# Differential attention: second softmax scaled by ScalarE and added by GpSimd, reciprocals by GpSimd, the output's transpose a stage later; band attention: one reciprocal per job

## The chip, the cores and the metric

The kernel runs on one core of a Trainium2 chip. The metric is device time in microseconds of one launch, as the median of several runs. A profile is one further execution, recorded instruction by instruction. The engines are TensorE (PE, with its weight loads PEld), VectorE (DVE), ScalarE (ACT), GpSimd (POOL) and SyncE (SP), which issues nearly all transfers. Each engine works through its own queue in order; semaphores tie the queues together.

## The reference

One encoder layer on x of shape (1, 1024, 1024) in float32. A half-step feed-forward comes first, then a mixer with two attention branches and gates, then a second half-step feed-forward and a norm. The change touches only the two attention branches. What they compute, cut to what matters:

```python
# band branch: 8 heads of 64, chunks of 64, own chunk and 8 to the left
sc = einsum(q, k) * d**-0.5 + bias          # band of 576 keys per chunk
p  = softmax(sc);  o = p @ v

# differential branch: 4 heads, two score maps each, 8 blocks of 128 queries
sc   = einsum('bqhrd,bkhrd->bhrqk', q, k) * d**-0.5 + t5_bias, chunk-causal
p    = softmax(sc)
attn = p[:, :, 0] - lam * p[:, :, 1]
o    = attn @ v                              # 128 value columns
o    = rms_norm(o, subln_g) * (1 - lambda_init)
```

## The kernel before

The feed-forwards and projections are matrix products in a Strassen-like form (seven products for eight), in a high and a low part of float32r each; they fill the time before 1077 us and after 1357 us. The attention lies between them, in one PSUM pool: two score tiles (`sc`, two banks each), two transpose tiles (`pt`), two result tiles (`pv`).

Attention work is cut into jobs. A band job is one head and two query blocks; 32 of them run first. A differential job is one head and one query block `i`, whose score width is `(i + 1) * 128`, from 128 to 1024 columns; 32 of them follow, 4 heads of 8 blocks. A job is a generator, and `run` (L811) steps the jobs as a pipeline: at each step a new job does its scores and softmax, the job of two steps before does its transposes, the one of three steps before its value product, and the one of four steps before its output transpose. The step only sets the order of the program text. The framework plans each engine's queue from that order, from what is ready in its own timing model, and from free buffers: a tile tag with `bufs=n` has n buffers, and an instruction that needs a new one cannot go into the queue before an old one is free.

A differential job before the change, line by line. L779/L780 are the two score products (high query times high and low keys). L787 adds the bias on VectorE and takes the row minimum, L789 is ScalarE's exp with the row sum `rs`. L922 and L924 are the reciprocals r1 and r2 on VectorE, L925 turns r2 into minus lambda times rs0/rs1, and L927 adds the second exp tile, scaled by r2, to the first. Two stages later L795 transposes the tile block by block, L97 (ScalarE) and L102 (VectorE) split it into high and low part (`whi`, `wlo`), and L943/L944 multiply with the values. L946 and L948 (ScalarE) take the two halves out of PSUM, scaled by r1; L949 (GpSimd) adds them to o1; L952 (VectorE) sums the squares; L139 (GpSimd) takes the power -1/2 and L955 (GpSimd) makes a diagonal `dg` of it. One stage later L958 multiplies o1 with dg on TensorE, which transposes and scales at once, and L99/L104 split the result into `y`.

A filler runs in between: every second job also does one 512-column piece of the band branch's output projection (`pb`, L128 to L130, times a gate tile `gl` in L892, stored by L893). The next head's queries, keys and values (`load_qkv`, L757) are loaded into the "big" buffers when the old ones come free.

The band job has the same softmax, then per query block a reciprocal on VectorE (L847) and a product with it on GpSimd (L848).

## Time and profile before

| | |
|---|---|
| median of 3 runs | 2159.53 us (2156.72 to 2159.69) |
| profiled execution | 2157.48 us, span of its instructions 2155.1 us |
| TensorE, VectorE, ScalarE, GpSimd busy | 96%, 68%, 45%, 9% of the span |
| band attention | about 1077 to 1187 us |
| differential attention | about 1187 to 1357 us |

Busy time is the time in which at least one instruction of the engine was under way. Matmuls overlap in the pipeline, so a busy TensorE isn't one at full pace. A wait names the instruction that waited and the one that released it.

### The profile page before, as it was taken

The numbers are of one execution on the slowest core, as the hardware profiler recorded it, in microseconds if no ns is written. First come the engines' busy times: TensorE is split into PE (matmuls) and PEld (weight loads), VectorE is DVE, ScalarE is ACT, GpSimd is POOL, SyncE is SP. The second block draws the span as 40 slices with busy tenths as digits, with TensorE's granted clock in tenths as the row PEclk, the third lists the DMA queues.
The fourth block names the chain that finished last, engine by engine and source line by source line (L and its number), as shares of the span: only waits on it lengthen the run. The fifth ranks groups of instructions, "written<-read, shape, count | busy, mean of one in ns | idle before, by whom it ended". The sixth has DMA issues, their size and how long they took to land.

```text
span 2155.1 us, 29016 instructions
## 1 busy us (share of the span) xinstructions
PE 2074.9 (96%) x10025; PEld 1730.3 (80%) x10025; DVE 1460.8 (68%) x2678; ACT 975.0 (45%) x1911; POOL 193.3 (9%) x290
## 2 busy tenths in 40 slices
PE   6999999999999999999999988898999999999997
PEld 5788888888888788899788877776788888888886
DVE  7666566577577756566488877777766656658566
ACT  5433333334446544444498665135433333334444
POOL 2120000000001000000066233201000000000001
PEclk9999999999999999999999999999999999999999
DMA  6653333294345544553682365614643333366344
GB/s 193 174 169 111 96 95 118 93 336 133 118 130 158 169 143 164 195 196 137 224 279 103 134 210 184 230 59 157 181 156 92 114 94 96 114 244 220 98 118 156
DMA packets 277572, 333.55 MB, mean 155 GB/s; under 512 B 15421, under 2 KB 168013, under 8 KB 277425
## 3 DMA queue, kind: packets, MB, share of 16 engines
q1 hardware_dynamic: 276096, 327.94, 46.8%
q0 software_dynamic: 1184, 3.24, 0.6%
q8 instruction: 79, 1.29, 0.3%
q14 instruction: 69, 0.56, 0.1%
q10 hardware_dynamic: 144, 0.52, 0.1%
HBM read 226.45 MB, written 105.19 MB: 154 GB/s over the span
## 4 chain that ended last, share of the span: by engine, by line
PE 80%; DVE 7%; DMA 5%; ACT 4%; issue 3%; SPq 1%; POOL 0%; ACTq 0%; DVEq 0%; POOLq 0%
PE prod L128 19%; PE prod L129 19%; PE prod L130 18%; PE po L129 6%; PE po L130 6%; PE po L128 6%; DVE wlo L102 2%; ACT whi L97 1%; ACT pm L789 1%; PE tr L205 1%; PE pb L128 1%; PE pb L130 1%; PE pb L129 1%; PE pt L795 1%; PE sc L779 1%
## 5 line engine op out<-in xcount | busy, mean ns | idle before, releaser
L129 PE MATMUL po<-wlo,whi 128*128 128x512 f32 x728 | 285.2, 392 | 5.5 <-DVE wlo L102 5.4
L130 PE MATMUL po<-whi,wlo 128*128 128x512 f32 x728 | 283.9, 390 | 0.0
L97 ACT CAST whi<-raw 128x512 fp32r<-128x512 f32 x200 | 124.4, 622 | 311.5 <-PE prod L129 244.4
L97 ACT CAST whi<-T 128x512 fp32r<-128x512 f32 x196 | 121.9, 622 | 249.7 <-PE prod L129 228.5
L97 ACT CAST whi<-B 128x512 fp32r<-128x512 f32 x178 | 110.8, 623 | 266.1 <-PE po L129 258.2
L113 DVE TENSOR_TENSOR c<-prod,c 128x512 f32<-128x512 f32 x190 | 131.1, 690 | 133.3 <-PE prod L130 122.3
L102 DVE TENSOR_TENSOR wlo<-raw,whi 128x512 fp32r<-128x512 f32 x200 | 138.6, 693 | 106.2 <-ACT whi L97 64.8
L102 DVE TENSOR_TENSOR wlo<-B,whi 128x512 fp32r<-128x512 f32 x178 | 122.4, 688 | 127.3 <-ACT whi L97 127.3
L128 PE MATMUL po<-whi 128*128 128x512 f32 x728 | 198.8, 391 | 0.4 <-DVE xc L507 0.3
L102 DVE TENSOR_TENSOR wlo<-T,whi 128x512 fp32r<-128x512 f32 x196 | 134.6, 687 | 92.5 <-ACT whi L97 91.6
L139 POOL TENSOR_TENSOR r<-v,neg_half 128x1 f32<-128x1 f32 x64 | 50.3, 790 | 1324.2 <-DVE v L180 1225.9
L129 PEld LDWEIGHTS po<-wlo,whi 128*128 128x128 f32 x728 | 136.9, 188 | 38.0 <-DVE wlo L102 9.8
L128 PEld LDWEIGHTS po<-whi 128*128 128x128 f32 x728 | 136.7, 189 | 29.9 <-ACT whi L97 1.4
L130 PEld LDWEIGHTS po<-whi,wlo 128*128 128x128 f32 x728 | 136.9, 188 | 28.2
L102 DVE TENSOR_TENSOR wlo<-N,whi 128x512 fp32r<-128x512 f32 x64 | 44.1, 689 | 113.2 <-PE prod L129 62.9
L102 DVE TENSOR_TENSOR wlo<-ha,whi 128x512 fp32r<-128x512 f32 x154 | 105.4, 684 | 9.0 <-ACT whi L97 9.0
L272 ACT COPY c<-prod 128x512 f32<-128x512 f32 x186 | 103.1, 586 | 11.2 <-DMA hA<-c 4.3
L97 ACT CAST whi<-ha 128x512 fp32r<-128x512 f32 x154 | 94.8, 615 | 16.9 <-PE prod L129 11.4
L789 ACT ACTIVATE pm<-pm,mn 128x640 f32<-128x640 f32 (+7 forms) x128 | 94.0, 736 | 11.9 <-DVE ri L924 6.3
L128 PE MATMUL prod<-A11h,whi 128*128 128x512 f32 x240 | 95.7, 399 | 2.6 <-ACT A11h L97 2.6
L128 PE MATMUL prod<-S1h,whi 128*128 128x512 f32 x240 | 94.1, 392 | 3.1 <-ACT S1h L97 2.1
L787 DVE CUSTOM_DVE_ANT_0 pm<-sc,nb 128x640 f32<-128x640 f32 (+7 forms) x128 | 87.9, 698 | 12.5 <-PE sc L780 5.9
(246 smaller groups left out, 5369.4 us busy)
## 6 DMA issues: line engine op xcount, KB each, us to landing
raw<-in_ffn_w_in_dram SPq DMA_DIRECT2D x98, 512.0 KB, 4.4
raw<-in_w_mix_in_dram SPq DMA_DIRECT2D x47, 512.0 KB, 4.5
ha<-hS SPq DMA_DIRECT2D x88, 256.0 KB, 2.7
hA<-c SPq DMA_DIRECT2D x66, 256.0 KB, 4.3
ha<-hA SPq DMA_DIRECT2D x66, 256.0 KB, 2.7
B<-in_ffn_w_out_dram SPq DMA_DIRECT2D x12, 1024.0 KB, 10.3
hS<-hs SPq DMA_DIRECT2D x44, 256.0 KB, 3.0
hS<-c SPq DMA_DIRECT2D x44, 256.0 KB, 4.5
```

The costliest lines, as they stand in the source:

```text
L97: nc.scalar.copy(out=hi, in_=src)
L102: (nc.gpsimd if on_pool else nc.vector).tensor_tensor(out=lo, in0=src, in1=h, op=ALU.subtract)
L113: nc.vector.tensor_tensor(out=out_, in0=a, in1=b, op=op)
L128: nc.tensor.matmul(ps, a[0], b[0], start=first, stop=False, skip_group_check=shared)
L129: nc.tensor.matmul(ps, a[0], b[1], start=False, stop=False, skip_group_check=shared)
L130: nc.tensor.matmul(ps, a[1], b[0], start=False, stop=last, skip_group_check=shared)
L139: nc.gpsimd.tensor_tensor(out=r, in0=v, in1=neg_half, op=ALU.pow)
L205: nc.tensor.transpose(tr[:, k, :], rows[:, k * P:(k + 1) * P], ident)
L272: nc.scalar.copy(out=self.held[name], in_=p)
L779: nc.tensor.matmul(sc[:, m, :wc], qs[:, h, c], ks[:, h, kc], start=True, stop=False)
L787: nc.vector.tensor_tensor_reduce(out=d3, in0=sc, in1=nb.rearrange("p (n w) -> p n w", n=n), scale=1.0, scalar=3e38, op0=ALU.add, op1=ALU.m ...
L789: nc.scalar.activation(out=dst, in_=dst, func=AF.Exp, bias=mn, scale=-1.0, accum_out=rs)
```

## The change

In the differential branch the two row sums share one tile, and one GpSimd instruction raises both to the power -1 (instead of two VectorE reciprocals). ScalarE scales the second exp tile by r2 in place and GpSimd adds it to the first (instead of one fused VectorE instruction). The reciprocals get a tag of their own with 6 buffers. The output's transpose (L958) moves one stage later, by a second `yield`, and `run` keeps five jobs alive instead of four. In the band branch the two row sums share a tile and are inverted by one VectorE reciprocal behind the second softmax; both GpSimd products follow it.

```diff
+    neg_one = const.tile([P, 2], F32, name="neg_one")
+    nc.vector.memset(neg_one, -1.0)
...
-            for step, job in enumerate(list(jobs) + [None] * 4):
+            for step, job in enumerate(list(jobs) + [None] * 5):
                 for g in [job] + live[::-1] if job else live[::-1]:
                     next(g, None)
-                live = (live + [job] if job else live)[-4:]
+                live = (live + [job] if job else live)[-5:]
...
+                rs = small.tile([P, 2], F32, tag="rs", bufs=4, name="rs")
                 for s, i in enumerate((i0, i1)):
                     w = (i - first[s] + 1) * P
                     sc, n = scores(qkv, h, i, first[s] * P, w)
                     pm = raw_tile([P, D], "pm")[:, :w]
-                    rs = small.tile([P, 1], F32, tag="rs", name="rs")
-                    softmax(sc, n, nb[:, h, WA - w:WA], pm, rs)
-                    ri = small.tile([P, 1], F32, tag="ri", name="ri")
-                    nc.vector.reciprocal(out=ri, in_=rs)
-                    nc.gpsimd.tensor_tensor(out=pm, in0=pm, in1=ri.to_broadcast([P, w]), op=ALU.mult)
+                    softmax(sc, n, nb[:, h, WA - w:WA], pm, rs[:, s:s + 1])
                     pms.append(pm)
+                ri = small.tile([P, 2], F32, tag="ri", name="ri")
+                nc.vector.reciprocal(out=ri, in_=rs)
+                for s, pm in enumerate(pms):
+                    nc.gpsimd.tensor_tensor(out=pm, in0=pm, in1=ri[:, s:s + 1].to_broadcast(list(pm.shape)), op=ALU.mult)
...
-                pr, rs = [], []
+                pr = []
+                rs = small.tile([P, 2], F32, tag="rs", name="rs")
                 for r in range(2):
                     sc, n = scores(qkv, r, i, 0, w)
                     pm = raw_tile([P, WB], "pm")[:, :w]
-                    s_ = small.tile([P, 1], F32, tag="rs", name="rs")
-                    softmax(sc, n, nb[:, WB - w:], pm, s_)
+                    softmax(sc, n, nb[:, WB - w:], pm, rs[:, r:r + 1])
                     pr.append(pm)
-                    rs.append(s_)
-                r1, r2 = (small.tile([P, 1], F32, tag="ri", name="ri") for _ in range(2))
-                nc.vector.reciprocal(out=r1, in_=rs[0])
-
-                nc.vector.reciprocal(out=r2, in_=rs[1])
-                nc.vector.scalar_tensor_tensor(out=r2, in0=r2, scalar=neg_lam, in1=rs[0],
+                ri = small.tile([P, 2], F32, tag="rj", bufs=6, name="ri")
+                nc.gpsimd.tensor_tensor(out=ri, in0=rs, in1=neg_one, op=ALU.pow)
+                r1, r2 = ri[:, 0:1], small.tile([P, 1], F32, tag="r2", name="r2")
+
+                nc.vector.scalar_tensor_tensor(out=r2, in0=ri[:, 1:2], scalar=neg_lam, in1=rs[:, 0:1],
                                                op0=ALU.mult, op1=ALU.mult)
-                nc.vector.scalar_tensor_tensor(out=pr[0], in0=pr[1], scalar=r2, in1=pr[0],
-                                               op0=ALU.mult, op1=ALU.add)
+                nc.scalar.activation(out=pr[1], in_=pr[1], func=AF.Copy, scale=r2)
+                nc.gpsimd.tensor_tensor(out=pr[0], in0=pr[0], in1=pr[1], op=ALU.add)
...
                 dg = small.tile([P, P], F32, tag="dg", bufs=2, name="dg")
                 nc.gpsimd.tensor_tensor(out=dg, in0=ident, in1=rsqrt(v).to_broadcast([P, P]), op=ALU.mult)
+                yield
                 yield
                 tr = ps.tile([P, 4, P], F32, tag="pt", bufs=2, name="try")
```

## Rows read from the trace of the kernel before

**Rows 1.** The page's busy time by engine: microseconds, share of the span, instructions.

```profile
PE 2074.9 (96%) x10025; PEld 1730.3 (80%) x10025; DVE 1460.8 (68%) x2678; ACT 975.0 (45%) x1911; POOL 193.3 (9%) x290
```

**Rows 2.** Busy time by stretch: the band part and the differential part. Columns: stretch, its length, then busy time (and instructions) of TensorE, its weight loads, VectorE, ScalarE and GpSimd, the granted TensorE clock (1.00 is 2.4 GHz), the DMA share and GB/s.

```profile
1077.00:1187.00 110.00, 102.33 (x734) 91.33 (x735) 96.92 (x311) 98.21 (x255) 74.21 (x93) 1.00 0.56 189
...
1187.00:1357.00 170.00, 147.02 (x872) 126.85 (x871) 133.51 (x410) 101.79 (x274) 55.64 (x100) 0.97 0.55 185
```

**Rows 3.** Waits of TensorE in the differential part: who waited for whom, microseconds in total, times, longest.

```profile
PE try L958 <- POOL dg L955: 4.6, 4, 2.4
PE pv L943 <- ACT o L948: 3.2, 6, 0.9
PE sc L779 <- DVE mn L787: 2.8, 5, 1.2
PE sc L779 <- DMA ks<-k: 2.2, 1, 2.2
PE pb L128 <- DVE gl L892: 2.2, 2, 1.6
PE try L958 <- DVE wlo L102: 2.1, 2, 1.8
PE try L958 <- DVE ri L925: 2.0, 2, 1.1
```

**Rows 4.** Waits of VectorE and ScalarE around the reciprocals, in the differential part.

```profile
ACT pm L789 <- DVE ri L924: 6.3, 9, 1.8
...
DVE ri L924 <- ACT o L948: 4.8, 5, 1.4
```

**Rows 5.** The end of the differential part in order of time, engine by engine: start, duration, engine, line, operation, tiles, shapes; in brackets the idle time before it and its releaser.

```profile
1330.89 0.19 ACT L789 ACTIVATION_READ_ACCUMULATOR pm<-pm,mn 128x1 f32 x1
...
1335.51 0.15 DVE L924 RECIPROCAL ri<-rs 128x1 f32<-128x1 f32 x1
1338.01 0.69 DVE L892 TENSOR_TENSOR gl<-pb,gl 128x512 f32<-128x512 f32 x1 [2.35 <-DMA gl<-g]
...
1339.55 1.27 DVE L927 SCALAR_TENSOR_TENSOR pm<-pm,ri 128x1024 f32<-128x1024 f32 x1
...
1353.90 0.49 PE L958 MATMUL try<-dg,o 128*128 128x128 f32 x2 [2.42 <-POOL dg L955]
```

**Rows 6.** VectorE's groups in the differential part, by shape: busy microseconds and mean ns of one, then idle time before them. L927 has eight widths of 4 jobs each (one of the narrowest lies before the stretch); the widest and the narrowest are shown.

```profile
L925 DVE SCALAR_TENSOR_TENSOR ri<-ri,neg_lam,rs 128x1 f32<-128x1 f32 x30 | 6.8, 227 | 0.2
...
L927 DVE SCALAR_TENSOR_TENSOR pm<-pm,ri 128x1024 f32<-128x1024 f32 x4 | 5.1, 1275 | 0.0
...
L922 DVE RECIPROCAL ri<-rs 128x1 f32<-128x1 f32 x30 | 4.7, 157 | 0.3
L924 DVE RECIPROCAL ri<-rs 128x1 f32<-128x1 f32 x30 | 4.6, 155 | 4.9 <-ACT o L948 4.8
...
L927 DVE SCALAR_TENSOR_TENSOR pm<-pm,ri 128x128 f32<-128x128 f32 x3 | 1.2, 394 | 0.0
```

**Rows 7.** ScalarE: the exp at its widest and narrowest in the differential part (busy, mean ns, idle before), and the one scaled copy from SBUF to SBUF in the program (a group over the whole span: shortest, median and longest ns, first and last start).

```profile
L789 ACT ACTIVATE pm<-pm,mn 128x1024 f32<-128x1024 f32 x8 | 9.2, 1147 | 1.1 <-DVE ri L924 0.9 <-DVE mn L787 0.2
...
L789 ACT ACTIVATE pm<-pm,mn 128x128 f32<-128x128 f32 x6 | 2.4, 404 | 1.6 <-DVE mn L787 1.6
...
L197 ACT ACTIVATE xc<-xc,r x12: 705/712/730, 682.1 to 2148.4; 128x512 f32<-128x512 f32 x12
```

**Rows 8.** GpSimd over the whole span: instructions with two tiles as input, by shape (busy, mean ns, idle before), and the power on one column (shortest, median and longest ns, first and last start).

```profile
L949 POOL TENSOR_TENSOR o<-o,o 128x128 f32<-128x128 f32 x32 | 14.7, 460 | 60.6 <-ACT o L948 60.6
L102 POOL TENSOR_TENSOR y<-ysum,y 128x256 fp32r<-128x256 f32 x16 | 11.8, 737 | 23.6 <-ACT y L97 23.6
...
L1000 POOL TENSOR_TENSOR mS<-mA,tA 128x512 f32<-128x512 f32 x4 | 5.5, 1386 | 22.5 <-DVE tA L113 22.5
...
L139 POOL TENSOR_TENSOR r<-v,neg_half x64: 544/560/2061, 7.4 to 2147.3; 128x1 f32<-128x1 f32 x64
```

**Rows 9.** The band part: the reciprocal (shortest, median and longest ns, first and last start) and TensorE's largest wait there.

```profile
L847 DVE RECIPROCAL ri<-rs x64: 144/158/166, 1078.7 to 1175.2; 128x1 f32<-128x1 f32 x64
...
PE pt L795 <- DVE wlo L102: 4.8, 15, 0.5
```

**Rows 10.** Two places of the differential part in order of time where GpSimd and VectorE meet: columns as in rows 5.

```profile
1291.81 0.45 POOL L949 TENSOR_TENSOR o<-o,o 128x128 f32<-128x128 f32 x1 [1.36 <-ACT o L948]
...
1291.96 0.32 DVE L925 SCALAR_TENSOR_TENSOR ri<-ri,neg_lam,rs 128x1 f32<-128x1 f32 x1
...
1332.86 1.15 DVE L927 SCALAR_TENSOR_TENSOR pm<-pm,ri 128x896 f32<-128x896 f32 x1
...
1333.02 1.40 POOL L139 TENSOR_TENSOR r<-v,neg_half 128x1 f32<-128x1 f32 x1 [0.41 <-DVE v L952]
```

**Rows 11.** Loads of a head's keys in the differential part: count, KB each, median microseconds from issue to landing.

```profile
ks<-k SPq DMA_DIRECT2D x3, 1024.0 KB, 8.9
kl<-kx SPq DMA_DIRECT2D x3, 1024.0 KB, 11.6
```

## The prediction

> **What bounds the kernel now.** I read the page's busy shares first: TensorE (PE) works 96% of the span and VectorE (DVE) 68% [rows 1]. As a mean over the whole program this says that TensorE is the limit, and that VectorE relief is worth little. The change touches only the attention part, so I next read the busy time by stretch [rows 2]. The band part (1077 to 1187 us) has TensorE at 102.3 of 110.0 us, ScalarE at 98.2 and VectorE at 96.9: three engines near their limit, 7.7 us of TensorE idle. The differential part (1187 to 1357 us) is different: TensorE 147.0 of 170.0 us, VectorE 133.5, ScalarE 101.8, GpSimd 55.6. No engine is full there. 23.0 us of TensorE idle time are what a change of order can win at most, apart from time in which TensorE counts as busy but runs at a poor pace.
>
> The third view is who ended TensorE's idle pieces in the differential part [rows 3]. The largest is the output's transpose (try, L958) waiting for GpSimd's diagonal dg, 4.6 us; then the value product (pv) waiting for ScalarE to empty its bank, 3.2 us; scores waiting for VectorE, 2.8 us; try behind VectorE, 2.1 and 2.0 us. Only the load of the next head's keys (2.2 us) and the gate tile (2.2 us, behind its load) have nothing to do with the arithmetic. So this stage waits on hand-overs between engines, not on one resource.
>
> The fourth view, waits of the other engines, shows a loop [rows 4]. The tag "ri" has 4 buffers and a job takes two of them: r1 stays taken until L948, three stages later in the pipeline. So VectorE's second reciprocal (L924) waits for an earlier job's L948, and ScalarE's exp waits for L924, which frees "rs" (4 buffers, two per job). The tail shows the cost best [rows 5]: the last exp's sum is read at 1331.08 (1330.89 + 0.19), but L924 runs at 1335.51, VectorE then stands 2.35 us for a gate load, and the combination L927 ends at 1340.82 (1339.55 + 1.27): 9.7 us after the exp, for work that itself takes about 1.8 us.
>
> **The change part by part.**
>
> *VectorE in the differential part.* L927 disappears: widths 128 to 1024 in equal steps, 0.394 us at the narrowest and 1.275 at the widest [rows 6], mean of the ends 0.835, times 32 jobs = 26.7 us. Both reciprocals disappear: 32 x (0.157 + 0.155) = 10.0 us. L925 stays. VectorE falls from 133.5 to about 96.8 us.
>
> *ScalarE.* It gains one scaled copy per job. The trace has no such copy at these widths; the exp on the same tile is the nearest row, 0.404 to 1.147 us, and the one scaled copy of 512 columns takes 0.712 us [rows 7], like the exp between. Taken: mean of the ends 0.776 x 32 = 24.8 us, so 126.6 us in all. Since neighbouring ScalarE instructions overlap by about 0.1 us, the lower bound is 21.6.
>
> *GpSimd.* It gains an add of two inputs per job. Such adds took 0.460 us at 128 columns, 0.737 at 256 and 1.386 at 512 [rows 8]. The slope between the first two is 0.277 us per 128 columns, so 1024 columns take 0.460 + 7 x 0.277 = 2.40 us, the mean is 1.43, and 32 of them 45.8 us. The power on 2 columns is bounded by the one on 1 column (median 0.56 us) and twice that; I take the first, as a single column costs more here than a column of a wide add: 32 x 0.56 = 17.9 us (upper 35.8). GpSimd goes from 55.6 to about 119.
>
> *The chain of a job* from exp's sum to the finished tile is now power 0.56, L925 0.23, scale up to 1.15, add up to 2.40: 4.3 us for the widest, plus hand-overs, against 0.16 + 0.16 + 0.23 + 1.27 = 1.8 before. It is longer, but no longer tied to an earlier job's L948: the new tag for the reciprocals has 6 buffers, one per job, and "rs" holds four jobs, not two. The transposes that read the tile come two stages later, and a stage is 170/32 = 5.3 us. So I cost the longer chain at nothing inside the stretch; without that cover it would cost 2.5 us per job. In the tail there is no cover: 1331.1 + 4.3 + some 0.5 of hand-overs gives 1335.9 against 1340.8, so even there it is 4.9 us earlier; I count 4.
>
> *The transpose one stage later.* dg is made a full stage (5.3 us) ahead of its reader. The longest such wait was 2.42 us, at the very end [rows 5], where no later job covers it. So of 4.6 us, 2.2 go. The waits of L958 behind VectorE (2.1 + 2.0) should go as well: they are the same delay with another releaser. A wait is added: dg has 2 buffers and now lives two stages, so GpSimd's next dg waits for L958 of two jobs before, and behind it queue the next job's power and add, and so ScalarE's scale. L958 is short, and the tile it needs is old by then; I count nothing, with up to 0.5 us per job if TensorE is late (16 us, in the range only through the rival below). o1 also stays in the 10 "temp" buffers a stage longer, so gate loads may start later: between 0 and a doubling of 2.2 us.
>
> *Band.* 32 of 64 reciprocals go, 0.158 us each [rows 9]: 5.1 us of VectorE. TensorE waits 4.8 us for VectorE's wlo there, which frees the transposes' bank. The first tile's GpSimd product now starts after the second softmax, one exp and its sum later (about 1 us, between the ends of [rows 7]), but is read two stages (2 x 110/32 = 6.9 us) later. Gain between 0 and 4.8 us; as ScalarE (98.2 of 110) is untouched, I take 1.
>
> *Sum for the differential part:* dg 2.2, try behind VectorE 4.1, tail 4, half of the 2.8 us in which scores wait for VectorE 1.4, and 1.3 for the granted clock, which is 0.97 in this stretch and 1.00 in the band [rows 2]; less 2 us for new hand-overs through ScalarE and GpSimd. That makes 11.0. With the band 12.0 us.
>
> *A rule against it.* GpSimd and VectorE exclude each other in the trace [rows 10]: a power that takes 0.544 us at its fastest took 1.40 while L927 ran, and ended 0.41 us after it (1334.42 against 1334.01). The other way, L925 took 0.32 us instead of 0.23 in the mean [rows 6] and ended with GpSimd's add (1292.28 and 1292.26). The Trainium skill says the same in "SBUF — State Buffer", section "Who interferes with whom": a VectorE instruction with two SBUF inputs and a GpSimd instruction that reads SBUF block each other for the whole instruction, whichever came first. By that rule alone the long adds would hold VectorE's L952 and L925 for their full length. What this would cost is the third rival below, from rows.
>
> **Rivals.**
>
> 1. *The idle time moves, the end does not.* Key loads of 1 MB land 8.9 us (ks) and 11.6 us (kl) after issue [rows 11], and are issued only when the previous head's scores have freed their buffers. Today the delayed older jobs fill that gap on TensorE; if they finish sooner, TensorE waits for the load. Three head changes at up to 3 us take back 9 of the 12: about 2156. For it: scores already wait 2.2 us for ks. Against: the tail has no load and keeps its 4 us.
>
> 2. *ScalarE becomes the bound (slower).* ScalarE works in order. Right behind the second exp it may stand for the power (0.56) and L925 (0.23) with two hand-overs, some 1.2 us, if nothing else is queued between. All 32 jobs: 38 us, so 126.6 + 38 = 165 us of ScalarE time. In the band ScalarE reaches 98.2/110 = 0.89; at that share the part needs 165/0.89 = 185 us, 15 more than now: about 2174. It decides from 0.89 x 170 - 126.6 = 25 us, or 0.77 us per job, on. Against: casts and older jobs' copies can stand between exp and scale.
>
> 3. *The exclusion (slower or same).* Adds fill 45.8 of some 158 us, a share of 0.29. If each L952 and L925 that meets one waits 0.9 us on average, that is 64 x 0.29 x 0.9 = 17 us, and VectorE comes to 114, still under its old 133.5. It takes 36.7 us, or 1.15 us per job, to eat all relief; if every L952 and half the L925 wait a whole add, 48 x 1.43 = 69 us bring VectorE to 166, at the band's share of 96.9/110 = 0.88 the part to 188, 18 us more: 2178.
>
> **How the numbers follow.** The profiled execution took 2157.48 us (span 2155.1 and 2.4 around it). 2157.5 - 12.0 = 2145.5. The median of the runs, 2159.53, is 2.05 above it, which gives 2147.5; I say 2147. Chances: the forecast 0.65 (own range 2137 to 2153: 22 us if nearly all idle time went, 6 if the band gives nothing and the new hand-overs cost twice), rival 1 0.18, rival 2 0.11, rival 3 0.06. A measurement here tells about 0.2%, 4.3 us, from no change. Rival 1 lies at the edge of that: I count 0.14 of it as same and 0.04 as faster. Half of rival 3 is mild enough to end as same. Faster 0.69, same 0.17, slower 0.14. The range 2136 to 2162 leaves out rival 2, the worse half of rival 3 and a little below.
>
> **What would show it.** Right: in the differential part VectorE at about 97 us, ScalarE about 125, GpSimd 110 to 125; TensorE's waits for dg nearly gone, the stretch 158 to 160 us long, the last combined tile about 5 us after the last exp. Wrong: a scaled copy that ScalarE waits over 0.8 us for, with VectorE's L925 as the releaser; L952 at over 1 us in the mean; waits of the scores for ks and kl that grow from 2 us to 8 or more.

## The result and the profile after

The changed kernel takes 2161.54 us (median), the kernel before 2157.77 in the runs beside it: ratio 1.0018, 95% interval 1.0011 to 1.0024. That is slower by 0.18%, inside the 0.2% that the prediction took as no change; the forecast was 12 us less. To see where the 12 us went, I cut the span at three points: the first score of the attention, the first exp of the differential part, the end of the last output transpose. Each profile is one execution; the changed kernel has two. Two executions of after_text (below), at a granted clock of 0.84 and 0.65 where its others had 0.98, are left out.

| us | up to the attention | band part | differential part | rest | span |
|---|---|---|---|---|---|
| before | 1076.9 | 106.8 | 170.7 | 800.7 | 2155.1 |
| after | 1075.4 | 108.8 | 170.7 | 806.4 | 2161.2 |
| after, second profile | 1076.1 | 108.8 | 168.8 | 803.8 | 2157.4 |

So the differential part, forecast 11 us shorter, is 0 to 2 us shorter; the band part, forecast 1 us shorter, is 2 us longer; and the rest, where nothing was edited, is 3 to 6 us longer. The two profiles of one kernel also show what a difference of 2 to 3 us between two profiles is worth: nothing.

The length of a part is TensorE's busy time plus its idle time. The two parts before, the same after, and the differential part in the second profile (columns as in [rows 2]):

```profile
1076.90:1183.70 106.80, 99.09 (x714) 88.47 (x715) 93.78 (x297) 95.93 (x246) 74.21 (x93) 1.00 0.58 195
1183.70:1354.40 170.70, 148.55 (x888) 128.29 (x886) 136.29 (x424) 103.81 (x283) 55.64 (x100) 0.98 0.53 179
```

```profile
1075.40:1184.20 108.80, 101.23 (x722) 89.03 (x722) 92.91 (x265) 97.12 (x248) 73.73 (x93) 1.00 0.55 186
1184.20:1354.90 170.70, 151.60 (x881) 130.69 (x879) 115.19 (x327) 123.54 (x313) 114.04 (x164) 0.95 0.52 175
```

```profile
1184.80:1353.60 168.80, 147.97 (x882) 126.78 (x880) 114.53 (x327) 123.31 (x313) 113.72 (x164) 0.98 0.52 178
```

The 2 us of the band part are no new waiting: 722 matrix products lie before the cut instead of 714, and TensorE's idle time is 7.6 us against 7.7. In the differential part its idle time is 19.1 and 20.8 us, against 22.1 before. The forecast of 11 us less, without the 1.3 for the clock, meant 9.7 us less idle time; it is 3.0 and 1.3 us less.

The page's busy line, answering [rows 1], and the second stretch of [rows 2]:

```profile
PE 2080.1 (96%) x10025; PEld 1733.5 (80%) x10025; DVE 1438.9 (67%) x2551; ACT 996.5 (46%) x1943; POOL 251.0 (12%) x354
```

```profile
1187.00:1357.00 170.00, 150.09 (x872) 129.45 (x871) 114.84 (x324) 122.65 (x309) 113.05 (x163) 0.95 0.53 181
```

In that stretch ScalarE (122.65) and GpSimd (113.05) are near their forecasts of 126.6 and 119, but VectorE (114.84) is far from its 96.8. TensorE's waits in the differential part, against [rows 3]:

```profile
PE sc L781 <- DVE mn L789: 5.3, 8, 2.1
PE pv L945 <- ACT o L950: 4.6, 7, 1.2
PE try L961 <- POOL dg L957: 3.7, 2, 2.5
PE try L961 <- DVE wlo L104: 2.5, 4, 1.1
PE pt L797 <- DVE wlo L104: 2.2, 2, 1.4
...
PE sc L782 <- DMA kl<-kx: 0.2, 1, 0.2
```

The wait for the diagonal fell only from 4.6 to 3.7 (2.5 of it is the last one, in the tail), scores wait 5.3 instead of 2.8 for VectorE, values 4.6 instead of 3.2 for ScalarE. Of the waits for key loads 0.2 us are left. Now the waits of the engines that make TensorE's inputs, in the same stretch:

```profile
ACT pm L929 <- DVE r L927: 5.6, 8, 1.5
...
DVE r L927 <- POOL ri L924: 9.2, 7, 2.2
DVE sq L954 <- POOL o L951: 7.1, 6, 2.0
...
POOL ri L924 <- ACT pm L791: 13.7, 13, 2.9
POOL pm L930 <- ACT pm L929: 11.6, 15, 1.5
POOL dg L957 <- PE try L961: 3.4, 3, 1.4
```

This is a chain through four queues. GpSimd's power (L924) stands for the exp; VectorE's r2 (L927) stands 9.2 us for the power; ScalarE's scaled copy (L929) stands for r2; GpSimd's addition (L930) stands for the copy; and the sum of o1 and o2 (L951), in the same GpSimd queue, comes later, so VectorE's sum of squares (L954) stands another 7.1 us, 4.7 of them while GpSimd is in such an addition. VectorE thus stands 16.3 us for GpSimd, where it stood 4.8 us for ScalarE in the old loop [rows 4]; ScalarE stands 5.6 us for r2, where it stood 6.3 us in that loop. The groups of VectorE and GpSimd by shape, against [rows 6, 8]:

```profile
L927 DVE SCALAR_TENSOR_TENSOR r<-ri,neg_lam,rs 128x1 f32<-128x1 f32 x31 | 11.5, 370 | 9.4 <-POOL ri L924 9.2
L954 DVE CUSTOM_DVE_ANT_0 sq<-o 128x128 f32<-128x128 f32 x32 | 11.4, 356 | 7.2 <-POOL o L951 7.1
...
L924 POOL TENSOR_TENSOR ri<-rs,neg_one 128x2 f32<-128x2 f32 x31 | 22.3, 720 | 14.1 <-ACT pm L791 13.7
...
L930 POOL TENSOR_TENSOR pm<-pm 128x1024 f32<-128x1024 f32 x4 | 9.5, 2372 | 0.6 <-ACT pm L929 0.6
```

r2 on one column takes 370 ns in the mean instead of 227, the sum of squares 356 instead of 287. The order of time shows why (start, duration, engine; idle in brackets):

```profile
1200.12 1.57 POOL L930 TENSOR_TENSOR pm<-pm 128x640 f32<-128x640 f32 x1
...
1200.53 1.17 DVE L927 SCALAR_TENSOR_TENSOR r<-ri,neg_lam,rs 128x1 f32<-128x1 f32 x1
...
1276.75 1.30 POOL L930 TENSOR_TENSOR pm<-pm 128x512 f32<-128x512 f32 x1
1276.83 1.36 DVE L954 CUSTOM_DVE_ANT_0 sq<-o 128x128 f32<-128x128 f32 x1 [1.42 <-POOL o L951]
```

Both VectorE instructions start while an addition runs and end at its end (1201.70 and 1201.69) or 0.14 us behind it (1278.19 and 1278.05). That is the exclusion of [rows 10], at full length. Of the 32 instances of r2 in the program 12 take over 0.35 us, and each of them ends within 0.03 us of the end of a GpSimd instruction; before, none of L925 takes that long.

The tail, against [rows 5]:

```profile
1330.91 0.19 ACT L791 ACTIVATION_READ_ACCUMULATOR pm<-pm,mn 128x1 f32 x1
...
1332.20 4.42 POOL L930 TENSOR_TENSOR pm<-pm 128x896 f32<-128x896 f32 x2
...
1346.72 0.60 PE L797 MATMUL pt<-ident,pm 128*128 128x128 f32 x4
```

The last combined tile is there at 1336.62 (1332.20 + 4.42, two additions), 5.5 us after the exp and 4.2 us earlier than before. But its transposes start at 1346.72, and the last output transpose comes half a microsecond later than before. TensorE still has older jobs to do until then, and does part of them at 1.2 GHz (granted clock 0.50 from 1335.6 to 1342.4 us).

### The profile page after: what moved, and what is told of

It is laid out like the page before. It is cut to its first block, busy times and chain, and to the rows that moved or that the text cites. A ratio compares the mean times of both kernels' runs of the same rounds, so it can differ in the third digit from the quotient of the medians.

```text
span 2161.2 us, 29040 instructions
## 1 busy us (share of the span) xinstructions
PE 2080.1 (96%) x10025; PEld 1733.5 (80%) x10025; DVE 1438.9 (67%) x2551; ACT 996.5 (46%) x1943; POOL 251.0 (12%) x354
## 5 line engine op out<-in xcount | busy, mean ns | idle before, releaser
L131 PE MATMUL po<-wlo,whi 128*128 128x512 f32 x728 | 284.8, 391 | 5.4 <-DVE wlo L104 5.3
L141 POOL TENSOR_TENSOR r<-v,neg_half 128x1 f32<-128x1 f32 x64 | 45.8, 719 | 1294.9 <-DVE v L182 1227.9
```

The costliest lines, as they stand in the source:

```text
L131: nc.tensor.matmul(ps, a[0], b[1], start=False, stop=False, skip_group_check=shared)
L141: nc.gpsimd.tensor_tensor(out=r, in0=v, in1=neg_half, op=ALU.pow)
```

## The experiments

Ratios are to the kernel before on the same chip, with 95% interval. "Band", "diff." and "rest" are the parts of the profiled execution, cut as above; "idle" and "clock" are TensorE's idle time and granted clock in the differential part (before: 22.1 and 0.98). Of the planned kernels, eight profiles have the band edit (the changed kernel's two among them), and their band part takes 108.8 to 109.4 us; in the eight without it, it takes 106.7 to 107.5. TensorE's idle time in it is 7.2 to 7.7 us in all of them but after_swap (10.5). Line numbers are those of each kernel.

| run | us | ratio | band | diff. | idle | clock | rest |
|---|---|---|---|---|---|---|---|
| band_only | 2168.38 | 1.0047 [1.0029, 1.0065] | 108.8 | 176.0 | 22.3 | 0.94 | 805.9 |
| arith_only | 2177.27 | 1.0095 [1.0073, 1.0117] | 109.4 | 189.1 | 31.2 | 0.93 | 804.9 |
| stage_only | 2165.29 | 1.0035 [1.0023, 1.0047] | 106.8 | 177.6 | 21.4 | 0.92 | 801.4 |
| no_comb | 2151.29 | 0.9977 [0.9964, 0.9989] | 106.8 | 160.5 | 14.1 | 0.97 | 802.2 |
| no_add | 2155.85 | 0.9994 [0.9984, 1.0003] | 108.8 | 164.1 | 17.4 | 0.98 | 806.3 |
| no_scale | 2164.54 | 1.0026 [1.0009, 1.0043] | 108.8 | 174.8 | 20.7 | 0.94 | 804.2 |
| no_band | 2161.95 | 1.0017 [1.0007, 1.0028] | 107.5 | 173.1 | 21.9 | 0.95 | 802.5 |
| no_band_vector_recip | 2154.18 | 0.9985 [0.9976, 0.9995] | 106.7 | 163.6 | 16.5 | 0.98 | 804.2 |
| vector_recip | 2164.31 | 1.0037 [1.0022, 1.0051] | 108.8 | 169.9 | 22.2 | 0.98 | 806.6 |
| tiles_stage | 2159.39 | 1.0006 [0.9995, 1.0017] | 106.7 | 166.1 | 16.3 | 0.97 | 803.8 |
| vector_recip_no_stage | 2164.34 | 1.0033 [1.0018, 1.0048] | 107.5 | 181.0 | 24.2 | 0.93 | 801.6 |
| before_swap | 2156.11 | 0.9992 [0.9977, 1.0006] | 107.5 | 170.8 | 18.5 | 0.95 | 798.5 |
| after_swap | 2169.41 | 1.0047 [1.0034, 1.0059] | 109.2 | 185.1 | 27.1 | 0.90 | 799.3 |
| before_text | 2158.52 | 1.0000 [0.9988, 1.0012] | 133.1 | 157.1 | 13.0 | 0.99 | 795.6 |
| after_text_again | 2190.33 | 1.0141 [1.0124, 1.0158] | 134.8 | 190.5 | 33.3 | 0.92 | 794.8 |
| vector_recip_text | 2176.42 | 1.0080 [1.0065, 1.0095] | 133.5 | 178.5 | 25.9 | 0.94 | 795.3 |

A longer part is not yet a longer wait. stage_only is 7 us longer in the differential part with no more idle time than the kernel before: TensorE is busy 156.2 us at a granted clock of 0.92, against 148.5 at 0.98, with the same number of products. Between the two profiles of the changed kernel, too, the busy time went from 151.6 us at 0.95 to 148.0 at 0.98.

**The parts alone.** band_only is the kernel before with the band part's edit; stage_only has nothing but the second `yield` behind dg (and the 5 steps in `run`); arith_only is the changed kernel without that:

```
                 dg = small.tile([P, P], F32, tag="dg", bufs=2, name="dg")
                 nc.gpsimd.tensor_tensor(out=dg, in0=ident, ...)
                 yield
-                yield
```

> The kernel before with only the band branch's part of the change (one reciprocal per job). Between the first score product and the end of the last output transpose the kernel before takes 277.5 us and the changed one 279.5; from there to the end 800.7 and 806.3. Theory A (the loss comes from another planned order behind the attention, which nearly any edit of the attention brings): attention 276 to 279 us, the rest 804 to 807, in all 2 to 5 us slower. Theory B (the loss comes from new waits in the differential branch): attention as before, the rest 800 to 802, in all within 1 us of before.

> The changed kernel without the extra stage (one yield, four live jobs); band and arithmetic as changed. Theory A (tiles are ready early and wait for TensorE; a stage more or less moves nothing): attention 278 to 282 us, the rest 804 to 807, in all 3 to 6 us slower than before. Theory B (the extra stage is what holds the changed kernel back, through dg's two buffers): attention 268 to 274 us. A third possibility, that the stage is needed as cover for GpSimd's longer queue: attention over 284 us.

> The kernel before with only the extra stage (L958 one stage later, five live jobs). Theory A: TensorE's waits for dg fall from 4.6 us to about 2.5, but other waits grow; attention 275 to 279 us. Theory B (dg is the wait that counts): attention 270 to 274 us.

TensorE's largest waits in the band part of band_only, and the largest in the differential part of arith_only:

```profile
PE pt L795 <- DVE wlo L102: 3.5, 8, 0.9
PE pt L795 <- POOL pm L849: 1.4, 3, 0.7
```

```profile
PE try L961 <- POOL dg L957: 11.8, 9, 2.3
```

With the band edit the wait for VectorE's wlo falls from 4.8 [rows 9] to 3.5 us, and a wait of 1.4 us of the transposes for GpSimd's product appears; the idle time of the band part stays as it was. As a whole band_only is 11.0 us slower than the kernel before, more than the changed kernel: its differential part is 5.3 us longer, at a clock of 0.94 and an idle time of 22.3 us, and its rest 5.2 us, though neither was edited. Its attention, 284.8 us, lies outside what either theory expected, and so does stage_only's, 284.3.

The arithmetic (with the band edit) makes the differential part 18 us longer, with 11.8 us of waits for the diagonal, and the stage alone makes it 7 us longer, but together they come out even. TensorE's idle time is 31.2 us with the arithmetic alone and 19.1 with the stage added. So the stage is not an extra on top: it pays for the longer way of the arithmetic.

**Relief without the detour.** no_comb is the kernel before without the second reciprocal, L925 and L927; the second softmax is left out of the result. r1 has 6 buffers of its own and the row sums have 8, so the loop of [rows 4] is gone too.

```
-                    s_ = small.tile([P, 1], F32, tag="rs", name="rs")
+                    s_ = small.tile([P, 1], F32, tag="rt", bufs=8, name="rs")
...
-                r1, r2 = (small.tile([P, 1], F32, tag="ri", name="ri") for _ in range(2))
+                r1 = small.tile([P, 1], F32, tag="rj", bufs=6, name="ri")
                 nc.vector.reciprocal(out=r1, in_=rs[0])
-                nc.vector.reciprocal(out=r2, in_=rs[1])
...
-                nc.vector.scalar_tensor_tensor(out=pr[0], in0=pr[1], scalar=r2, in1=pr[0],
-                                               op0=ALU.mult, op1=ALU.add)
```

> The kernel before without the second reciprocal, L925 and L927: the second softmax is left out of the sum (its exp still runs), and r1 has 6 buffers of its own. VectorE loses about 36 us of work in the differential part, and no other engine gets any. Theory A (TensorE and the path behind the transposes set the length): the differential part stays at 166 to 171 us, so attention 273 to 278 us. Theory B (VectorE's relief is worth what was forecast, and only the new work of ScalarE and GpSimd ate it): attention 262 to 268 us.

```profile
1182.90:1343.40 160.50, 146.37 (x888) 128.36 (x886) 105.57 (x327) 102.86 (x283) 46.85 (x100) 0.97 0.57 189
```

With a relief at least as large (L925 goes too) and nothing put on ScalarE and GpSimd, the differential part takes 160.5 us, 10.2 less: about the 11 that the prediction summed. TensorE's idle time falls by 8.0 us. In this one planned order the relief, freed buffers included, brings about what the sum said; that points to the price of the new way as the wrong term.

**Which engine takes it back.** In no_add ScalarE writes its copy into the first tile and GpSimd's addition is left out; in no_scale the copy is left out.

```
-                nc.scalar.activation(out=pr[1], in_=pr[1], func=AF.Copy, scale=r2)
-                nc.gpsimd.tensor_tensor(out=pr[0], in0=pr[0], in1=pr[1], op=ALU.add)
+                nc.scalar.activation(out=pr[0], in_=pr[1], func=AF.Copy, scale=r2)
```

> The changed kernel without GpSimd's addition: ScalarE writes its scaled copy of the second tile into the first tile, which the transposes read (the sum of the two softmaxes is left out). The order power, L927, scaled copy, transposes stays. Differential part of the changed kernel: 170.7 us, of which 8.5 are clock shortfall. Theory A (GpSimd's adds are what eats the relief: their 45.8 us, the power that queues behind them, and VectorE standing while they run): VectorE's L927 and L954 fall back to 230 and 290 ns, the wait of L927 for the power (9.2 us) is gone, the part takes 160 to 163 us, whole run 2149 to 2153. Theory B (ScalarE's scaled copies in order behind the power are what eats it): the part stays at 168 to 171 us, whole run 2158 to 2162. Theory C (the combined tile is in any case 8 us too early for TensorE, and the back half paces it): no change in the part, 169 to 171, and VectorE's shorter instructions come back as idle VectorE.

> The changed kernel without ScalarE's scaled copy (the second softmax is added unscaled; the factor of L927 is computed and not used). Theory B (ScalarE in order behind the power): ScalarE falls from 122.7 to about 98 us in the part, the values' waits for o1 (4.6 us) and the scores' for VectorE's minimum fall, the part takes 160 to 163 us, whole run 2149 to 2153. Theory A (GpSimd): adds and powers stay, so the part stays at 167 to 171 us, whole run 2157 to 2162. Theory C: 169 to 171 in both runs. If each gives 4 to 6 us, the two engines share the loss.

VectorE's r2 and sum of squares, first in no_add, then in no_scale:

```profile
L954 DVE CUSTOM_DVE_ANT_0 sq<-o 128x128 f32<-128x128 f32 x32 | 9.1, 284 | 1.7 <-POOL o L951 1.5
L927 DVE SCALAR_TENSOR_TENSOR r<-ri,neg_lam,rs 128x1 f32<-128x1 f32 x32 | 8.3, 259 | 8.1 <-POOL ri L924 8.0
```

```profile
L927 DVE SCALAR_TENSOR_TENSOR r<-ri,neg_lam,rs 128x1 f32<-128x1 f32 x32 | 25.0, 780 | 3.9 <-POOL ri L924 3.7
L954 DVE CUSTOM_DVE_ANT_0 sq<-o 128x128 f32<-128x128 f32 x31 | 12.3, 398 | 2.9 <-POOL o L951 2.8
```

Without the additions both instructions fall back to about their old length, and the part is 5 to 7 us shorter than in the changed kernel, just above Theory A's range, the run above its 2149 to 2153; the wait for the power stays at 8 us, against its expectation. Without the copies, 24.7 us of them on ScalarE, the part is not shorter at all; at 174.8 us it lies above what either theory expected. But the relief does not come alone, so the run does not show what ScalarE's time is worth by itself: the additions then follow the power at once, meet r2, and r2 takes 780 ns: 25.0 - 6.8 = 18 us more of VectorE than [rows 6]. Of its 21 instances over 0.35 us, 19 end within 0.02 us of an addition's end, so this is the exclusion; the copies had put a distance between the two.

**Band and power.** no_band gives the changed kernel its old band part; no_band_vector_recip and vector_recip make the reciprocals on VectorE, without and with the band edit:

```
-                nc.gpsimd.tensor_tensor(out=ri, in0=rs, in1=neg_one, op=ALU.pow)
+                nc.vector.reciprocal(out=ri, in_=rs)
```

> The changed kernel with the band part as before (one reciprocal and one product behind each softmax). The run of the band edit alone took 2.0 us more in the band part (108.8 against 106.8). Theory A (that loss is the late product of the job's first tile, for which the transposes wait): band part back to 106.8 us, and the whole run 2 us shorter, 2157 to 2160, if the order behind the attention stays as it is in the changed kernel (806 us). Theory B (the loss goes with any change of the planned order): band part stays at 108.8. The differential part should be 168 to 171 in both; if it moves by more than 3 us, its length hangs on how the band part hands over to it.

> As the run before it, and the differential part's two reciprocals as one VectorE instruction on 2 columns instead of GpSimd's power. VectorE gains 32 x about 0.16 = 5 us, GpSimd loses 32 x 0.72 = 23 us, and the chain exp to combined tile loses one change of engine. Theory A (the power, queued behind the previous job's add, diagonal and product, holds ScalarE's copies: L927 waits 9.2 us for it): the part falls by 4 to 8 us, whole run 2150 to 2154, faster than before. Theory B (VectorE's relief is what counts): VectorE's 5 us come back, the part is 0 to 3 us longer, 2158 to 2162.

> The changed kernel with one edit: the differential part's two reciprocals as one VectorE instruction on 2 columns instead of GpSimd's power (band edit kept). Theory A (the power in GpSimd's queue is what costs the change its gain: it takes 32 x 0.72 = 23 us of GpSimd and holds back the sums of o1 and o2, which came 1.11 us after ScalarE instead of 0.57): the differential part falls from 170.7 us to 161 to 165, the run to 2153 to 2157. Theory B (the 9.5 us between the two runs without the band edit came from the order that each kernel happened to get, or from the clock): the part stays at 168 to 173 us, the run at 2159 to 2163.

The band part does go back (107.5 and 106.7), but with it only the place of the cut: no_band's run is not the 2 us shorter that Theory A expected (2161.95). The power is undecided here: the same edit shortens the differential part by 9.5 us (173.1 to 163.6) without the band edit, and changes nothing (169.9 against 170.7 and 168.8) with it. no_band_vector_recip is faster than both kernels, by 0.15% than the one before, inside the 0.2%; and this pair shows that it may owe that to its order.

**Tiles, stage, second profile.** tiles_stage has before's arithmetic on VectorE, with one reciprocal on two columns in six buffers and the extra stage; vector_recip_no_stage is no_band_vector_recip without the stage; after_again is the changed kernel.

> The kernel before with the changed kernel's tiles and its extra stage, but with all arithmetic on VectorE: one reciprocal of 2 columns per job in 6 buffers of its own, the exp sums of a job in one tile, and the scaled addition L927 of before. The band part as before. VectorE is relieved by only 32 x about 0.15 = 5 us. Theory A (a job's r1, held until the values' copies three stages later, is what delays L924 and so the exp; freeing it is enough): the differential part takes 160 to 166 us, the run 2150 to 2155. Theory B (VectorE's 26.7 us in L927 are what the run without the combination won): the part stays near the 177.6 us of the extra stage alone, 172 to 178, the run 2159 to 2166.

> The kernel with the old band part and VectorE's reciprocals, with the output's transpose back one stage earlier. Theory A (the longer way through ScalarE and GpSimd needs the extra stage, whoever makes the reciprocals): TensorE waits 6 us or more for the diagonal, the part is 172 to 185 us, the run 2162 to 2172. Theory B (the 11.8 us of waits for the diagonal in the kernel without the extra stage came from the power in GpSimd's queue): the waits for it stay under 5 us, the part is 163 to 169, the run 2153 to 2158.

> The changed kernel once more, unchanged, for a second profile: how far the length of a part and the granted clock in it differ between two executions. If the low clock of 0.95 in the differential part belongs to this kernel's order, the part is again 169 to 172 us at 0.94 to 0.96; if it is chance, the part may come out at 163 to 167 at 0.97 or more.

tiles_stage takes 166.1 us, at the upper end of Theory A's range, and as a whole no different from before (forecast there: faster). So taking the loop of [rows 4] away may be worth some microseconds, no more. Taking the stage away again costs 17.4 us (181.0 against 163.6), as it did with the power (189.1 against 170.7), though the waits for the diagonal are 5.3 us, less than expected.

**The order alone.** The planner lays out the queues anew after each edit. before_swap and after_swap change only the order in which two instructions stand in the text:

```
+                nc.vector.reciprocal(out=r2, in_=rs[1])
                 nc.vector.reciprocal(out=r1, in_=rs[0])
-                nc.vector.reciprocal(out=r2, in_=rs[1])
```

```
-                for s, pm in enumerate(pms):
+                for s, pm in reversed(list(enumerate(pms))):
                     nc.gpsimd.tensor_tensor(out=pm, in0=pm, in1=ri[:, s:s + 1]...
```

> The kernel before, with the two reciprocals of a job in the other order in the program's text (r2's first). No work is added or taken away; but the planner then lays out the queues anew in the differential part (some 350 lines of TensorE's order differ, none in the band part). Theory A (the length of the differential part hangs on which planned order a kernel happens to get, by as much as on its work): the part differs from 170.7 us by 4 us or more, in either direction, and the run by more than 0.2% from 2157. Theory B (differences of that size come from the work of each edit): the part takes 168 to 173 us, the run 2155 to 2160.

> The changed kernel, with the two products of a band job in the other order in the program's text (second tile first). No work is added or taken away; some 520 lines of TensorE's order differ, in both parts. Theory A (planned order by chance): the differential part differs by 4 us or more from the 168.8 to 170.7 us of the changed kernel's two profiles, as the one reciprocal edit did between 173.1 and 163.6 without the band edit. Theory B (the work decides): 167 to 172 us, the run 2158 to 2164, or 1 to 2 us more for the first tile's product, which is still later now.

Before does not mind (170.8). The changed kernel's differential part grows to 185.1 us, by 14 to 16 us, without any work added, and the rest falls to 799.3. In the differential part TensorE's idle time is 27.1 us and its clock 0.90, and 28 products that lay before the cut now lie behind it; but both parts together grow as well, to 294.3 us from 279.5 and 277.5:

```profile
1185.30:1370.40 185.10, 158.01 (x909) 138.46 (x907) 126.35 (x331) 126.69 (x319) 114.63 (x165) 0.90 0.49 163
```

So between planned kernels, one difference of some 10 us in this part proves little, and the 3 to 6 us in the rest need no cause in the edited lines: these kernels range from 798.5 to 806.6 there.

**A coarser order.** The last runs switch off the planner's timing model:

```
-    with _tile.TileContext(nc, schedule_with_timeline_sim=True) as tc:
+    with _tile.TileContext(nc, schedule_with_timeline_sim=False) as tc:
```

The expectations call this the order of the text. That says too much: the traces show the framework still moving instructions past each other, by a coarser rule. Nor do these kernels share one order. Counted as the fewest of the attention's 1600 matrix products that must be moved to turn one order of TensorE into the other, before_text and after_text_again differ by 259, as much as planned kernels do (before and before_swap by 228, before and after by 461). Only after_text_again and vector_recip_text are close, with 25.

> The kernel before, with the planner switched off: each engine's queue stands in the order of the program's text, everywhere. The work is the same. Longer than before by an unknown amount; it is the measure for the run that follows, whose queues differ from this one's by the edit alone.

> The changed kernel with the planner switched off, to be compared with the run before it. Theory A (VectorE's relief is a gain as such, and the planned order is what took it back): the differential part is 8 us or more shorter than there, the band part within 1 us. Theory B (the longer way through GpSimd and ScalarE takes the relief back in any order): the differential part is within 4 us of that one or longer, the band part 1 to 4 us longer, as the first tile's product is late in any order.

> The changed kernel in the order of the text once more: the first profile of it fell into an execution in which the granted clock was 0.84 over the whole program (0.77 to 0.79 in the attention), so its lengths can't be compared with the kernel before in the order of the text (differential part 157.1 us, band part 133.1). Its undisturbed times were 2192.5 and 2193.9 us. Theory A (the longer way through GpSimd and ScalarE costs in any order): the differential part takes 175 to 185 us at a clock near that of the kernel before, ScalarE waits some 20 us for L927 and VectorE some 25 us for the power. Theory B (the loss lies elsewhere in the program): the part is within 5 us of 157.

> The changed kernel in the order of the text, with one reciprocal of 2 columns on VectorE instead of GpSimd's power, all else equal: the two queues' orders differ by this edit alone. Theory A (the power is what makes the chain late: it stands behind the job's older additions on GpSimd, VectorE's L927 stands for it and ScalarE's scaled copy for that): the waits of L927 for the power (26.9 us) go, those of the scaled copy for L927 (21.4 us) fall below 12, and the run is 10 us or more shorter than the 2193 of the changed kernel in this order. Theory B (the detour over ScalarE and GpSimd itself, additions above all, is the loss): the run stays within 5 us of 2193.

after_text's two other times are 2192.52 and 2193.86 us; after_text_again is the same kernel, and its profile is used here. The kernel before takes as long as with the planner (ratio 1.0000), distributed otherwise: 157.1 us in the differential part, 133.1 in the band part. In this order the changed kernel needs 190.5 us for the differential part, 33 more, and 32 more as a whole (30 by the ratios). Of the 33 us 20.3 are idle time of TensorE (13.0 to 33.3), the others busy time at a clock of 0.92 instead of 0.99. First before_text, then after_text_again, then vector_recip_text; waits of TensorE for VectorE's casts, then of ScalarE and VectorE, in the differential part:

```profile
PE pt L795 <- DVE y L104: 2.6, 5, 1.3
...
PE try L958 <- DVE wlo L102: 0.5, 2, 0.2
...
ACT pm L789 <- DVE ri L924: 2.3, 5, 1.0
...
DVE sq L952 <- POOL o L949: 4.7, 7, 1.5
...
DVE ri L924 <- ACT o L948: 4.4, 9, 1.0
```

```profile
PE pt L797 <- DVE y L106: 10.4, 7, 3.3
PE try L961 <- DVE y L106: 4.7, 4, 1.9
PE try L961 <- DVE wlo L104: 4.6, 5, 1.5
PE pt L797 <- DVE wlo L104: 4.2, 4, 2.8
...
ACT pm L929 <- DVE r L927: 21.4, 25, 1.8
...
DVE r L927 <- POOL ri L924: 26.9, 21, 3.1
DVE sq L954 <- POOL o L951: 26.0, 18, 2.4
```

```profile
PE try L961 <- DVE y L106: 6.9, 3, 3.1
PE try L961 <- DVE wlo L104: 5.7, 7, 1.6
PE pt L797 <- DVE y L106: 4.4, 8, 1.3
...
ACT pm L929 <- DVE r L927: 7.7, 12, 1.2
...
DVE sq L954 <- POOL o L951: 24.6, 21, 4.3
```

It is the same chain as in the planned kernel, and here it reaches TensorE. VectorE stands 52.9 us for GpSimd, ScalarE 21.4 us for r2, and TensorE's transposes wait 23.9 us for VectorE's casts, against 3.1 in before_text. Of TensorE's waits for VectorE (29.1 us with the others) 25.4 us follow a stand of VectorE for GpSimd at most three instructions earlier in VectorE's queue; in the planned changed kernel that holds for only 3.4 of 10.0 us. One link in order of time (after_text_again): power, r2 and scaled copy, the last two with their waits:

```profile
1305.28 0.69 POOL L924 TENSOR_TENSOR ri<-rs,neg_one 128x2 f32<-128x2 f32 x1
...
1306.01 0.50 DVE L927 SCALAR_TENSOR_TENSOR r<-ri,neg_lam,rs 128x1 f32<-128x1 f32 x1 [1.20 <-POOL ri L924]
...
1306.60 0.72 ACT L929 ACTIVATE pm<-pm,r 128x512 f32<-128x512 f32 x1 [0.65 <-DVE r L927]
```

Taking the power alone off GpSimd gives back 12.0 us of the part (190.5 to 178.5) and 13.9 of the whole, as Theory A expected: the waits of the copies for r2 fall from 21.4 to 7.7, and TensorE's idle time from 33.3 to 25.9. These two orders are close, so this is nearly the price of the one hop. The remaining 21.4 us of the part (178.5 against 157.1) stand with the detour of the combination, the band edit, the stage and the other order together; the 24.6 us for which VectorE stands for the sum of o1 and o2, 11.0 of them while GpSimd is in an addition, are the largest row of it. These were not separated.

## Why the prediction was wrong, step by step

- **What bounds the kernel** held as far as tested: hand-overs, not one full engine. Relief of VectorE, with the freed buffers, was worth 10.2 us in no_comb's order, against the 11.0 of the sum.
- **VectorE, 96.8 forecast, 114.8 measured.** Two errors of size. The 36.7 us were sums of durations; neighbouring VectorE instructions overlap, and with each moment given to the one that started first, L927 and the reciprocals filled only 30.1 us. And 11.5 us came back, in the same count: r2 4.7, the sum of squares 2.8, the casts of weights 2.0, the rest 2.0. Together that is the 18.7 us by which the busy time fell. r2 and the sum of squares are the exclusion, as no_add shows.
- **ScalarE** +24.8 forecast, +24.7 measured as the sum of 31 copies; its busy time rose by 20.9, as neighbours overlap (the lower bound given was 21.6). **GpSimd's additions** 45.8 forecast, 45.6 measured. **Powers** 17.9 forecast, 22.3 measured for 31: two columns cost 0.72 us, not the 0.56 of one, within the bound given.
- **The chain, 4.3 us and hand-overs, costed at nothing, and the "2 us for new hand-overs": this is the step that failed.** The tile itself was not late: from exp to combined tile 5.1 us in the mean, before even 8.2. The prediction asked who waits for the tile. It did not ask who is queued behind the instructions that wait: casts, minima and sums of squares behind r2 on VectorE, exps and o1 copies behind the scaled copy on ScalarE, the sum of o1 and o2 behind power and addition on GpSimd. In the planned order that is 9.2 + 7.1 us on VectorE and 5.6 on ScalarE. The sum took the waits of TensorE for VectorE to fall by 5.5 us; they are 10.1 us before and 10.0 and 10.5 after (waits over 0.1 us, parts cut as above), and those for ScalarE went from 3.5 to 4.8 and 4.7. That the chain costs time is shown for one hop in the coarser order, 12.0 us for the power; the 33 us of the whole change there hold a change of order as well. In the planner's own order its price is not shown, and how much of the missing 11 us is order stays open, since order alone moved the part by up to 16 us.
- **Diagonal and try, 2.2 + 4.1.** Fell by 0.9 and 1.6. The extra stage did its work, but for the longer way: without it the part is 17 to 18 us longer in two pairs, 12.1 and 7.7 of them idle time of TensorE.
- **The tail, 4.** The tile came 4.2 us earlier, close to the forecast 1335.9. The end did not: TensorE was behind by more than that. The step took the tile as the end of the chain; the chain of waits had to be followed to TensorE's next free moment.
- **Scores behind VectorE, 1.4, and the clock, 1.3.** The first wait grew from 2.8 to 5.3. The clock was 0.95 and 0.98 in two executions, 0.98 before (cut as above); nothing was gained.
- **The band, -1, measured +2.0 in length and -0.1 in idle time.** The 2 us are where the cut falls. The first tile's late product was costed at nothing because it is read two stages later; transposes wait for it 1.4 us, and that takes back the 1.3 by which the wait for wlo fell.
- **The rest** was taken as unchanged; it ran 3 to 6 us longer, without an edit there; order alone moves it by as much (after_swap).
- **The rivals.** Key loads (1): no, 0.2 us. ScalarE (2): the mechanism is there, at 5.6/32 = 0.18 us per job in the planned order and 21.4/32 = 0.67 in the other, below the 0.77 from which it was to decide. Exclusion (3): there, some 7 us on r2 and the sum of squares, not the 17 estimated. The Trainium skill's rule in "SBUF — State Buffer", section "Who interferes with whom", agrees with the two places shown. None of the three decided alone, and what share the second and third took was not separated. The list of signs had no row for VectorE standing for GpSimd, 16.3 us in the planned order and 52.9 in the other.

## What to carry to other kernels

An instruction that waits on an in-order queue costs what stands behind it, not what it makes: before moving a small step to another engine, list for each queue that it passes what comes next there. Three short hops (power, r2, copy) between three busy engines stand here for one instruction of at most 1.3 us, and the first of them cost 12 us of 190 where it could be tested by itself. And where a planner lays out the queues anew, a change of nothing may move the time by as much as the edit: measure a swap without work beside the edit, or compare two kernels whose orders the traces show to be close, before a difference of half a percent is given a cause. And split the length of a part into TensorE's idle and busy time: some of these differences were not waits, but the same products at a lower granted clock.

## What the hardware showed unexpectedly

A VectorE instruction on one column stood 1.17 us, to the end of a GpSimd addition that it met. GpSimd's power on two columns takes 0.70 us (median), against 0.16 us (mean) for VectorE's reciprocal of two. The granted clock of the same kernel in the same part was 0.95 in one execution (0.95 x 170.7 = 162 us at full speed) and 0.98 in another (165 of 168.8): three hundredths of clock, some 5 us, moved the part by 1.9. TensorE was busy 3.6 us less in the second and idle 1.7 us more. This stretch, which waits on other engines, did not lengthen by what its clock lost.
